# One batch for each group of eight partitions, and rotary tables filled for each tile

## The chip, the cores and the metric

The kernel runs on one core of a Trainium2 chip. The metric is the device time of one execution in microseconds (us); smaller is better. Three timed runs of the kernel before gave 161.45, 161.63 and 161.63 us, median 161.63 us. A difference below about 0.2% can't be told from none here.

The core's engines that matter are VectorE (DVE in the profile), which does all the arithmetic; SyncE (SP), which issues most of the transfers; GpSimd (POOL), which issues three of them; and the 16 DMA engines, which carry every transfer between device memory and the on-chip memory of 128 partitions.

## The reference

The input `x` is float32 of shape (16, 512, 16, 64): batch, position, head, element. Only the first half of each 64-element row is rotated, by a table that depends on the position alone; the second half is passed through.

```python
batch, seq, heads, dim = x.shape            # 16, 512, 16, 64
half_dim = dim // 2                         # 32
x1, x2 = x[..., :half_dim], x[..., half_dim:]
cos = cos[None, :, None, :]                 # (1, 512, 1, 32)
sin = sin[None, :, None, :]
a, b = x1[..., :16], x1[..., 16:]
rotated_first  = a * cos[..., :16] - b * sin[..., :16]
rotated_second = a * sin[..., :16] + b * cos[..., :16]
return np.concatenate([rotated_first, rotated_second, x2], axis=-1)
```

So 33.55 MB are read and 33.55 MB are written, and only the first 16 columns of each table are used.

## The kernel before

**Tiles.** A "run" is K = 16 consecutive positions of one batch: 16 x 16 heads x 64 elements x 4 bytes = 65,536 contiguous bytes. A batch has 32 runs (`PB`). The 512 runs make T = 4 tiles of 128 runs, one run per partition. In the kernel before, run number `128t + p` of the whole input lies in partition `p` of tile `t`, so a tile is one contiguous piece of 8.39 MB: four batches of 32 partitions each. The names `load`, `store` and `rows` move tile `t` (or a range of its 16 positions) to or from slot `t % 3` of `ring`. Three slots hold four tiles: tile 3 goes into slot 0 when tile 0 has been stored.

**Tables.** Position run `r` of a batch needs table run `r` (16 positions x 16 columns, of cos and of sin). GpSimd loads the two tables into every fourth partition of `stage` (lines 63 and 64). `stream_shuffle` (line 73) then spreads them within each group of 32 partitions: partition `32q + j` of `spun` gets table run `8q + (j mod 8)`. Because in this layout every batch occupies 32 partitions in order, partition `p` always needs table run `p mod 32`, whatever the tile. The loop at lines 78 to 80 collects the 32 runs in order in `packed` with four copies, and the loop at lines 82 to 86 writes the table four times (once per group of 32 partitions), with each column pair doubled so that one instruction can multiply 32 columns. This is done once, for all tiles.

**Arithmetic.** `rotate(t, lo, hi)` does positions `lo` to `hi` of a tile with four VectorE instructions: x1 * sin into `b_t` (line 96), x1 * cos in place (line 97), a subtraction (line 98) and an addition (line 101). Half a tile (KC = 8 positions) is one `rotate`; the second half of tile 2 is cut in two at KM = 13.

**Order.** VectorE runs its instructions in program order. SP's queue has, in this order: load 0, load 1, first half of load 2, store 0, second half of load 2, load 3, store 1, store 3. Each waits for what it needs, and holds up those behind it: store 0 for the rotation of tile 0, load 3 for store 0, store 1 for an added dependency on `near`, the first piece of the second half of tile 2. Store 2 goes through GpSimd's queue. All of them are carried by the same 16 DMA engines.

Of the kernel before, what the change touches and what calls it, by code (L numbers as in the profile page):

```python
# [1 line left out]

# [4 lines left out]


@with_exitstack
def kernel(  # L10
    ctx: ExitStack,
    tc: tile.TileContext,
    x: bass.AP,
    cos: bass.AP,
    sin: bass.AP,
    out: bass.AP,
):
    nc = tc.nc
    fp32 = mybir.dt.float32
    P = 128  # L20
    B, S, H, D = x.shape
    Q = D // 4
    HF = D // 2

    K = 16
    T = B * S // (P * K)
    PB = S // K
    REP = P // PB  # L30
    R = H * D
    NS = 3
    KC = K // 2
    KM = 13

    xf = x.rearrange("b s h d -> (b s h d)").rearrange("(t p f) -> t p f", t=T, p=P)
    of = out.rearrange("b s h d -> (b s h d)").rearrange("(t p f) -> t p f", t=T, p=P)
    cosf = cos.rearrange("(p k) j -> p (k j)", k=K)
    sinf = sin.rearrange("(p k) j -> p (k j)", k=K)

    const_pool = ctx.enter_context(tc.tile_pool(name="const", bufs=1))
    b_pool = ctx.enter_context(tc.tile_pool(name="bp", bufs=1, space=bass.MemoryType.PSUM))


    ring = const_pool.tile([P, NS, K, H, D], fp32)
    stage = const_pool.tile([P, 2, K, HF], fp32)
    spun = const_pool.tile([P, 2 * K, Q], fp32)
    packed = const_pool.tile([PB, 2 * K, Q], fp32)
    table = const_pool.tile([P, 2, K, 2, Q], fp32)

    def rows(t, lo, hi):
        return ring[:, t % NS, lo:hi].rearrange("p k h d -> p (k h d)")

    def load(t, lo=0, hi=K):
        return nc.sync.dma_start(out=rows(t, lo, hi), in_=xf[t, :, lo * R : hi * R])

    def store(t, lo=0, hi=K, queue=nc.sync):
        return queue.dma_start(out=of[t, :, lo * R : hi * R], in_=rows(t, lo, hi))  # L58


    nc.vector.memset(stage[:, :, :, 0:Q], 0.0)  # L61
    spread = stage.rearrange("(j b) t k i -> j b t (k i)", b=REP)
    nc.gpsimd.dma_start(out=spread[:, 0, 0], in_=cosf)  # L63
    nc.gpsimd.dma_start(out=spread[:, 0, 1], in_=sinf)  # L64
    load(0)
    load(1)
    load(2, 0, KC)

    PQ = PB // REP
    nc.vector.stream_shuffle(  # L73
        out=spun[:],
        in_=stage.rearrange("p t k j -> p (t k) j")[:, :, 0:Q],
        mask=[j % PQ * REP for j in range(PB)],
    )
    for q in reversed(range(REP)):
        n = PQ * (q + 1)
        nc.vector.tensor_copy(out=packed[0:n], in_=spun[q * PB : q * PB + n])  # L80

    for r in range(REP):
        nc.vector.tensor_copy(  # L83
            out=table[r * PB : (r + 1) * PB].rearrange("p t k c j -> p (t k) c j"),
            in_=packed.unsqueeze(2).to_broadcast((PB, 2 * K, 2, Q)),
        )
    C = table[:, 0].rearrange("p k c j -> p k (c j)")
    Sn = table[:, 1].rearrange("p k c j -> p k (c j)")

    def rotate(t, lo, hi):  # L90
        x1 = ring[:, t % NS, lo:hi, :, 0:HF]
        c = C[:, lo:hi].unsqueeze(2).to_broadcast((P, hi - lo, H, HF))
        s = Sn[:, lo:hi].unsqueeze(2).to_broadcast((P, hi - lo, H, HF))
        b_full = b_pool.tile([P, KC, H, HF], fp32, name="b_t")
        b_t = b_full[:, 0 : hi - lo]
        nc.vector.tensor_mul(out=b_t, in0=x1, in1=s)  # L96
        nc.vector.tensor_mul(out=x1, in0=x1, in1=c)  # L97
        nc.vector.tensor_sub(  # L98
            out=x1[:, :, :, 0:Q], in0=x1[:, :, :, 0:Q], in1=b_t[:, :, :, Q:HF]
        )  # L100
        return nc.vector.tensor_add(  # L101
            out=x1[:, :, :, Q:HF], in0=x1[:, :, :, Q:HF], in1=b_t[:, :, :, 0:Q]
        )

    rotate(0, 0, KC)
    rotate(0, KC, K)
    store(0)
    load(2, KC, K)
    load(3)
    rotate(1, 0, KC)  # L110
    rotate(1, KC, K)
    behind_loads = store(1)
    rotate(2, 0, KC)
    near = rotate(2, KC, KM)
    rotate(2, KM, K)
    store(2, queue=nc.gpsimd)

    tc.add_manual_dep(
        behind_loads.ins,
        near.ins.name,  # L120
        mybir.DependencyInfo(mybir.DependencyClass.Sync, mybir.DependencyReason.DATA),
        reason="the store follows the loads at the DMA engines",
    )
    rotate(3, 0, KC)
    rotate(3, KC, K)
    store(3)


# [1 line left out]
_INS = ['x', 'cos', 'sin']  # L130
_OUTS = [((16, 512, 16, 64), 'float32')]


# [23 lines left out]
```

## Time and profile before

| what | value |
| --- | --- |
| timed runs, median of 3 | 161.63 us |
| the profiled execution, first to last instruction (span) | 159.5 us |
| share of the span in which VectorE is busy | 71% |
| bytes moved, mean rate over the span | 67.24 MB, 422 GB/s |
| VectorE's longest wait for a transfer: for the sin table | 14.4 us |
| VectorE's only wait for a load of `x`: for load 0 | 1.9 us |
| last VectorE instruction (line 101) ends | 131.2 us |
| first rotation starts | 23.0 us |

The page of a profile divides the span by engine and lists groups of instructions, transfers and waits. A "DMA share" is the mean busy share of the 16 DMA engines in a stretch of time; packets are counted where they start, so a short stretch can show more than 1. "To landing" is the time from the issue of a transfer to its completion mark, and holds the time it spent queued behind others. The span is 2.1 us shorter than the timed median; that part lies outside the first and last instruction.

### The profile page before, as it was taken

Reading aid. Unit: us, or ns where it says so; the run is one execution under the profiler, and the core shown is the slowest. Engines: PE = TensorE matmul, PEld = TensorE weight load, DVE = VectorE, ACT = ScalarE, POOL = GpSimd, SP = SyncE. Lnnn points to the kernel's source line nnn. Section 1 sums busy time; section 2 is a strip of 40 time slices with the busy share of each in tenths; the row PEclk is TensorE's granted clock in tenths of the full one; section 3 lists DMA queues with packets and bytes.
Section 4 is the critical chain, followed back from the end, with each engine's and each line's share of the span. In section 5 each row is a group of like instructions: output and inputs, shape, how many; then the busy total and the mean of one; then the engine's idle time right before and its main releaser. Section 6 shows DMA issues by size and latency. Waiting matters only on the chain.

```text
span 159.5 us, 115 instructions
## 1 busy us (share of the span) xinstructions
DVE 112.9 (71%) x47; POOL 1.9 (1%) x7
## 2 busy tenths in 40 slices
DVE  1000959999999999999999999999999990000000
POOL 3000000000000000000000000010000000000000
DMA  7969979899699699699996996996996996998966
GB/s 263 542 263 542 444 345 526 362 427 526 271 493 551 263 526 526 263 395 427 493 526 263 526 526 263 526 526 263 526 526 263 526 510 279 526 427 362 526 263 263
DMA packets 1360, 67.24 MB, mean 422 GB/s; under 512 B 176, under 2 KB 176, under 8 KB 208
## 3 DMA queue, kind: packets, MB, share of 16 engines
q1 hardware_dynamic: 1152, 58.72, 85.7%
q0 software_dynamic: 208, 8.52, 12.4%
HBM read 33.69 MB, written 33.55 MB: 422 GB/s over the span
## 4 chain that ended last, share of the span: by engine, by line
DVE 61%; DMA 14%; issue 5%; DVEq 1%
DVE b_t L96 22%; DVE ring L97 22%; DMA ring<-in_x_dram 14%; DVE ring L101 10%; DVE ring L98 7%; DVEq L152 1%; DVEq L96 0%
## 5 line engine op out<-in xcount | busy, mean ns | idle before, releaser
L96 DVE TENSOR_TENSOR b_t<-ring,table 128x4096 f32<-128x4096 f32 (+2 forms) x9 | 35.6, 3959 | 2.1 <-DMA ring<-in_x_dram 1.9
L97 DVE TENSOR_TENSOR ring<-ring,table 128x4096 f32<-128x4096 f32 (+2 forms) x9 | 35.6, 3950 | 0.3
L98 DVE TENSOR_TENSOR ring<-ring,b_t 128x2048 f32<-128x2048 f32 (+2 forms) x9 | 18.4, 2050 | 0.3
L101 DVE TENSOR_TENSOR ring<-ring,b_t 128x2048 f32<-128x2048 f32 (+2 forms) x9 | 18.4, 2043 | 0.0
L73 DVE LOAD_MASK_SELECT spun<-stage x1 | 0.0, 14 | 14.4 <-DMA stage<-in_sin_dram 14.4
L83 DVE COPY table<-packed 32x1024 f32<-32x1024 f32 x4 | 2.7, 684 | 0.1
L58 POOL DMA_DIRECT2D out_dram<-ring x1 | 0.6, 559 | 101.7 <-DVE ring L101 101.7
L80 DVE COPY packed<-spun 32x512 f32<-32x512 f32 (+3 forms) x4 | 1.7, 416 | 0.1
L61 DVE MEMSET stage<- 128x512 f32 x1 | 0.5, 485 | 0.9 <-PEq L141 0.9
L73 DVE STREAM_SHUFFLE spun<-stage 128x512 f32<-128x512 f32 x1 | 0.7, 722 | 0.0
L63 POOL DMA_DIRECT2D stage<-in_cos_dram x1 | 0.6, 642 | 1.3 <-DVE stage L61 1.3
L64 POOL DMA_DIRECT2D stage<-in_sin_dram x1 | 0.5, 532 | 0.0
L141 POOL MEMSET const-bfloat16-1.0<- 128x1 bf16 x1 | 0.1, 101 | 0.0
L141 POOL MEMSET const-float32-0.0<- 128x1 f32 x1 | 0.1, 98 | 0.2 <-issue 0.2
L141 POOL MEMSET const-float32-1.0<- 128x1 f32 x1 | 0.1, 98 | 0.0
L141 POOL MEMSET const-uint8-127<- 128x1 uint8 x1 | 0.1, 98 | 0.0
## 6 DMA issues: line engine op xcount, KB each, us to landing
ring<-in_x_dram SPq DMA_DIRECT2D x2, 4096.0 KB, 40.7
stage<-in_cos_dram POOLq DMA_DIRECT2D x1, 64.0 KB, 8.9
stage<-in_sin_dram POOLq DMA_DIRECT2D x1, 64.0 KB, 13.3
ring<-in_x_dram SPq DMA_DIRECT2D x3, 28.9
out_dram<-ring SPq DMA_DIRECT2D x3, 27.4
out_dram<-ring POOLq DMA_DIRECT2D x1, 39.5
```

The costliest lines, as they stand in the source:

```text
L58: return queue.dma_start(out=of[t, :, lo * R : hi * R], in_=rows(t, lo, hi))
L61: nc.vector.memset(stage[:, :, :, 0:Q], 0.0)
L63: nc.gpsimd.dma_start(out=spread[:, 0, 0], in_=cosf)
L64: nc.gpsimd.dma_start(out=spread[:, 0, 1], in_=sinf)
L73: nc.vector.stream_shuffle(out=spun[:], in_=stage.rearrange("p t k j -> p (t k) j")[:, :, 0:Q], mask=[j % PQ * REP for j in range(PB)],)
L80: nc.vector.tensor_copy(out=packed[0:n], in_=spun[q * PB : q * PB + n])
L83: nc.vector.tensor_copy(out=table[r * PB : (r + 1) * PB].rearrange("p t k c j -> p (t k) c j"), in_=packed.unsqueeze(2).to_broadcast((PB, ...
L96: nc.vector.tensor_mul(out=b_t, in0=x1, in1=s)
L97: nc.vector.tensor_mul(out=x1, in0=x1, in1=c)
L98: nc.vector.tensor_sub(out=x1[:, :, :, 0:Q], in0=x1[:, :, :, 0:Q], in1=b_t[:, :, :, Q:HF])
L101: return nc.vector.tensor_add(out=x1[:, :, :, Q:HF], in0=x1[:, :, :, Q:HF], in1=b_t[:, :, :, 0:Q])
L152: with _tile.TileContext(nc) as tc:
```

## The change

The distribution of the runs over the partitions changes. Partition `8b + i` of tile `t` now holds run `8t + i` of batch `b`: each tile holds eight runs of all 16 batches, and eight neighbouring partitions belong to one batch. Seen from device memory, a tile is no longer one piece of 8.39 MB but 16 pieces of 524,288 bytes, whose starts lie 2,097,152 bytes apart. The transfer's pattern on the memory side has an outer count of 16 and an inner count of 8, where it had one count of 128.

Tile `t` now needs table runs `8t` to `8t + 7`, repeated in every group of eight partitions. That is what `spun` holds in its partitions `32t` to `32t + 31`. The copies into `packed` are dropped, and `fill(t)` copies the quarter of `spun` that tile `t` needs into all four groups of 32 partitions of a table; two tables take turns. `fill(0)` and `fill(1)` stand ahead of the first rotation, `fill(2)` after store 1, `fill(3)` after store 2. KM goes from 13 to 9, so the instruction that store 1 waits for, `near`, does one position instead of five.

```diff
-    KM = 13
+    KM = 9
 
-    xf = x.rearrange("b s h d -> (b s h d)").rearrange("(t p f) -> t p f", t=T, p=P)
-    of = out.rearrange("b s h d -> (b s h d)").rearrange("(t p f) -> t p f", t=T, p=P)
+    xf = x.rearrange("b (t i k) h d -> t b i (k h d)", t=T, k=K)
+    of = out.rearrange("b (t i k) h d -> t b i (k h d)", t=T, k=K)
...
-    packed = const_pool.tile([PB, 2 * K, Q], fp32)
-    table = const_pool.tile([P, 2, K, 2, Q], fp32)
+    table = const_pool.tile([P, 2, 2, K, 2, Q], fp32)
...
-        return nc.sync.dma_start(out=rows(t, lo, hi), in_=xf[t, :, lo * R : hi * R])
+        return nc.sync.dma_start(out=rows(t, lo, hi), in_=xf[t, :, :, lo * R : hi * R])
...
-        return queue.dma_start(out=of[t, :, lo * R : hi * R], in_=rows(t, lo, hi))
+        return queue.dma_start(out=of[t, :, :, lo * R : hi * R], in_=rows(t, lo, hi))
...
-    for q in reversed(range(REP)):
-        n = PQ * (q + 1)
-        nc.vector.tensor_copy(out=packed[0:n], in_=spun[q * PB : q * PB + n])
-
-    for r in range(REP):
-        nc.vector.tensor_copy(
-            out=table[r * PB : (r + 1) * PB].rearrange("p t k c j -> p (t k) c j"),
-            in_=packed.unsqueeze(2).to_broadcast((PB, 2 * K, 2, Q)),
-        )
-    C = table[:, 0].rearrange("p k c j -> p k (c j)")
-    Sn = table[:, 1].rearrange("p k c j -> p k (c j)")
+    def fill(t):
+        for q in range(REP):
+            nc.vector.tensor_copy(
+                out=table[q * PB : (q + 1) * PB, t % 2].rearrange(
+                    "p t k c j -> p (t k) c j"
+                ),
+                in_=spun[t * PB : (t + 1) * PB]
+                .unsqueeze(2)
+                .to_broadcast((PB, 2 * K, 2, Q)),
+            )
 
     def rotate(t, lo, hi):
         x1 = ring[:, t % NS, lo:hi, :, 0:HF]
+        C = table[:, t % 2, 0].rearrange("p k c j -> p k (c j)")
+        Sn = table[:, t % 2, 1].rearrange("p k c j -> p k (c j)")
...
+    fill(0)
+    fill(1)
     rotate(0, 0, KC)
...
     behind_loads = store(1)
+    fill(2)
     rotate(2, 0, KC)
...
+    fill(3)
     rotate(3, 0, KC)
```

In the program as built, VectorE's eight copies of `fill(2)` and `fill(3)` stand between the rotations of tiles 1 and 2, and all eight stand ahead of `near`. The number and the order of the transfers on SP's and GpSimd's queues are as before.

## The prediction

> **What bounds the kernel now.** I read the page's parts 1 and 3 first: who is busy, and how full the transfer engines are.
>
> ```profile
> span 159.5 us, 115 instructions
> ...
> DVE 112.9 (71%) x47; POOL 1.9 (1%) x7
> ...
> q1 hardware_dynamic: 1152, 58.72, 85.7%
> q0 software_dynamic: 208, 8.52, 12.4%
> ...
> out_dram<-ring SPq DMA_DIRECT2D x3, 27.4
> out_dram<-ring POOLq DMA_DIRECT2D x1, 39.5
> ```
>
> The two queues' packets fill 85.7 + 12.4 = 98.1% of 16 engines' span: 156.5 of 159.5 us. VectorE is busy for 71%. So the DMA engines are the bound, and only 3.0 us of the span (start and end) are not theirs. One tile's transfer (8.39 of the 58.72 MB that took 0.857 x 159.5 = 136.7 us) costs 19.5 us alone. The last row shows what sharing costs: store 2 ran beside store 1 on the same engines and took 39.5 us from issue to landing.
>
> Then the rate by stretches, each with its start and end, busy time of DVE and POOL, the clock, the DMA share and GB/s:
>
> ```profile
> 22.00:51.00 29.00, 27.80 (x9) 0.00 (x0) 1.00 1.00 434
> 51.00:72.00 21.00, 20.86 (x6) 0.00 (x0) 1.00 1.00 424
> ...
> 101.00:132.00 31.00, 29.92 (x11) 0.56 (x1) 1.00 1.02 440
> 132.00:144.00 12.00, 0.00 (x0) 0.00 (x0) 1.00 1.01 437
> ```
>
> Loads alone (first row), store 0 (second) and stores from two queues (the last two) all go at 424 to 440 GB/s with the engines full: some 27 GB/s for each of 16, whatever the direction. Something fixed on each engine's path sets that pace. A faster kernel would need it to rise, or the 3.0 us to shrink.
>
> Last the timeline (start, duration, engine, line), for VectorE's table work and its slack:
>
> ```profile
> 16.56 1.77 DVE L80 COPY packed<-spun 32x512 f32<-32x512 f32 x4
> 18.36 2.78 DVE L83 COPY table<-packed 32x1024 f32<-32x1024 f32 x4
> 22.99 4.43 DVE L96 TENSOR_TENSOR b_t<-ring,table 128x4096 f32<-128x4096 f32 x1 [1.85 <-DMA ring<-in_x_dram]
> ...
> 98.86 32.68 SPq L58 DMA_DIRECT2D out_dram<-ring  x2
> ...
> 104.58 0.56 POOL L58 DMA_DIRECT2D out_dram<-ring  x1 [101.70 <-DVE ring L101]
> ```
>
> VectorE has its table 1.85 us before load 0 is in, and store 1 is issued at 98.86 us, 2 us before the loads ahead of it are done (the second store of that row is store 3, at 131.2 us).
>
> **The change, part by part.**
>
> Tables ahead of the first rotation: four copies into `packed` and four into `table` go (16.56 to 21.14, 4.6 us); eight of the second kind come, at 2.78 / 4 = 0.695 us with its gap, 5.6 us. They end at 22.1 us, still before load 0 (22.9). Cost nothing; cover left 0.8 us. If load 0 came at once, the price would be 1.0 us.
>
> `fill(2)` and `fill(3)`: eight copies more, 5.6 us on VectorE, all ahead of `near`. Against that `near` shrinks from five positions to one. The multiplications take 4.433 us for 4096 elements and 1.767 for 1536, so 1.04 ns an element and 0.17 fixed; 512 elements take 0.70. The additions (2.287 for 2048, 0.953 for 768) give 0.42 for 256. So `near` takes 2 x 0.70 + 2 x 0.42 + gaps, 2.3 us, instead of 98.86 - 90.22 = 8.6. Store 1 would be issued at 98.86 + 5.6 - 6.3 = 98.1 us: not later. The cut of tile 2 costs nothing in sum, with the same instructions and the same elements. Store 3 is issued 5.6 us later, at 136.8; stores 1 and 2 keep the engines full until 144, so that is hidden by about 7 us. Behind it on SP's queue stands only the end. At an unchanged transfer pace VectorE's additions are all covered; with no cover they are 6.6 us, which makes 168.
>
> Issuing: the same five loads and four stores in the same order, with a pattern of two counts. No row shows such an issue. SP's rows are 0.33 to 0.43 us each; I bound the change by -0.1 and +0.4 us apiece and take +0.2. Only load 0's is ahead of everything; later ones lie under transfers under way. POOL's issue (0.56 us) is bounded alike, and lies under store 1.
>
> Transfers: the same bytes in the same packets of 65,536, but each DMA engine gets one outer entry of 16, thus partitions 8b to 8b+7 and one batch. No row shows that assignment's pace. From below: no dearer, 19.5 us a tile. A gain beyond that is excluded by the engines being full at one pace in every stretch, except at the start (load 0 took 22.2 us against 19.5; a gain of 1 us there is the most I allow). From above: if engines meet pairwise on one path to the partitions, each pair shares as stores 1 and 2 shared engines (39.5 us for a tile): twice 19.5 everywhere. Between ends so far apart, the question is whether the 27 GB/s belong to the engine or to the group of partitions it reaches. I take the latter, as a judgement: the pace is the same for reading device memory and for writing it, which puts the limit at the other end of the path or in the engine; it is that of an assignment in which no engine stands in another's way; and no engine has idle time from which a new one could be better.
>
> [...]
>
> **Sum for the likeliest case.** 2 x 156.5 = 313 us if all pairs meet all the time. Less what falls out of step. Engines receive their work within one issue, 0.43 us, against 9.8 us for four packets (half a tile): 4% apart at the start, 6 us saved. And where load 3 and store 2 are under way together (two tiles, 39 us of work, 78 doubled), one engine may read while its partner writes; I take a third of that stretch's 39 us loss as saved, 13 us, between bounds of 0 and 39. So 313 - 6 - 13 = 294 in transfers, 3.0 us start and end, 2.1 us outside the span (161.63 - 159.5): 299 us. Its own range is 255 to 318: above, nothing saved (313 + 5.1); below, pairs that are out of step for four tenths of the work, 156.5 x (0.6 x 2 + 0.4) + 5.1 = 255. VectorE doesn't bind: load 0 lands at about 41 instead of 22.4, and from there VectorE's 113 + 6.6 us of work lie in 300.
>
> **The rivals.**
>
> Pairs fall out of step. One engine of a pair is favoured and gets its first four packets through alone; its partner is then half a tile behind, and they use different partition groups from there on. For it: nothing forces two engines to stay in step. Against it: both have equal work and start within 0.43 us. Price: 9.8 us once, 171 us, when they never meet again; 8 x 9.8 = 78 us, 240, when each of eight tile transfers begins in step. Middle 205. A milder loss elsewhere, as in device memory with its batches 2,097,152 bytes apart, would fall in the same stretch.
>
> The pace is the engine's own. Then partition neighbours don't matter, and what is left is VectorE's covered additions and 0.2 us of issue: 161.8 us, between 160.6 (the start gains 1 us) and 162.5. For it: the equal pace with one queue or two, loads or stores, is what an engine-bound kernel shows as well. Against it: nothing in the profile; it needs the path to any group of partitions to carry two engines' streams, 54 GB/s. From that rate on it decides. That the descriptor side ignores the new pattern and keeps the old assignment has the same price. This is the case on the other side: not slower.
>
> VectorE becomes the bound. Its work begins when load 0 is in (22.9) and ends 108.3 us later now (131.2); with 5.6 more, store 3 is issued at 136.8 and its 19.5 us end at 156.3 at the earliest, under the present 159.5. So only the 168 of lost covers, 2%, counted in the range of the first rival.
>
> **How the numbers follow.** Paired engines 0.70; out of step or a milder loss (163 to 255) 0.20; the engine's own pace 0.10. The predicted time is the first's, 299 us. The range reaches down to 195 and up to 322: that leaves out the last case (0.10), the lower part of the second (0.06) and a little above. A difference under 0.2% can't be told from none: of the last case's 0.10, 0.04 go to faster, 0.03 to within 0.2%, 0.03 to slower. So faster 0.04, same 0.03, slower 0.93.
>
> **What would show it.** Load 0's landing, and with it the first rotation: near 41 us for pairs in step, near 32 for one half late, 23 for no loss. The mean rate over the span: about 226 GB/s (67.24 MB in 297 us) against 422, with the DMA share still near 1, since engines that wait for a path count as busy. VectorE's share near 40%, with long waits for loads. The table copies should be sixteen of 0.68 us, and `near` about 2.3 us long. It is wrong if load 0 lands as before, or if the rate falls in the stores alone, which would put the loss in device memory's writes and not in the partitions.

## The result, and the profile after

The changed kernel takes 289.45 us (median of 6 runs, 285.83 to 295.25) against 161.63. Two of the six runs (290.25 and 295.25) count as slow, over 1.5% above the fastest, so the ratio is taken from the other four (mean 287.8 us): 1.78, 95% interval 1.773 to 1.788. The predicted time was 299 us. The profiled execution took 289.96 us, 288.2 of them in the span.

From the page of the changed kernel, parts 1, 3, 5 and 6 (busy time and share of the span; packets, MB and share of 16 engines; the groups of instructions; microseconds from issue to landing at the end):

```profile
DVE 119.5 (41%) x55; POOL 1.9 (1%) x7
...
DMA packets 1361, 67.25 MB, mean 233 GB/s; under 512 B 176, under 2 KB 176, under 8 KB 208
...
q1 hardware_dynamic: 1152, 58.72, 89.3%
q0 software_dynamic: 208, 8.52, 7.6%
...
L96 DVE TENSOR_TENSOR b_t<-ring,table 128x4096 f32<-128x4096 f32 (+2 forms) x9 | 35.6, 3959 | 84.0 <-DMA ring<-in_x_dram 83.8
...
L79 DVE COPY table<-spun 32x1024 f32<-32x1024 f32 x16 | 11.0, 684 | 0.4
...
out_dram<-ring SPq DMA_DIRECT2D x3, 67.5
```

The same bytes in as many packets (65,536 bytes each, 32,768 for the halves of load 2), and the engines' packets still fill 96.9% of the span (89.3 + 7.6). So the engines hardly rest; each packet takes longer (5.0 to 5.1 us against 2.42 in loads alone). VectorE, whose share fell from 71% to 41%, now waits 83.8 us for loads where it waited 1.9. Its work rose by 6.6 us, as worked out (119.5 against 112.9).

By stretches of the changed kernel (start and end, length, DVE and POOL busy, clock, DMA share, GB/s):

```profile
5.00:100.00 95.00, 47.91 (x25) 0.00 (x0) 1.00 0.99 206
105.00:155.00 50.00, 25.55 (x12) 0.00 (x0) 1.00 1.01 233
160.00:175.00 15.00, 13.89 (x8) 0.14 (x1) 1.00 0.99 210
175.00:207.00 32.00, 0.00 (x0) 0.41 (x1) 1.00 0.97 311
207.00:232.00 25.00, 24.77 (x8) 0.00 (x0) 1.00 1.07 352
235.00:285.00 50.00, 0.00 (x0) 0.00 (x0) 1.00 0.91 201
```

Loads alone (first row) go at 206 GB/s, less than half of 434 before; stores from SP's queue alone (last row) at 201. The second row is store 0 and then the second half of load 2, one behind the other in SP's queue. From 175 us, when store 2 is issued on GpSimd's queue, to 207, when load 3 lands, a load and a store are under way from two queues, at 311. From 207 to 232, when store 2 lands, only stores 1 and 2 are under way, still from two queues, and it is 352. In the trace 216 of the 240 packets of 65,536 bytes that start in the first stretch last 5.0 to 5.1 us, against 2.42 before; of those in the two stretches with two queues, 29 of 152 and 59 of 134 last 2.42 to 2.45 again.

Last the chain of waits of the changed kernel (start, length, what) and the first piece of tile 2 that store 1 waits for:

```profile
0.74 44.36 DMA ring<-in_x_dram
```

```profile
160.50 0.70 DVE L96 TENSOR_TENSOR b_t<-ring,table 128x512 f32<-128x512 f32 x1 [29.68 <-DMA ring<-in_x_dram]
...
162.74 0.59 SPq L57 DMA_DIRECT2D out_dram<-ring  x1
```

Load 0 takes 44.4 us from issue to landing (22.2 before; the prediction had 41), and `near` takes 162.74 - 160.50 = 2.2 us; the 2.3 of the prediction were right, but VectorE had stood still for 29.7 us before it.

### The profile page after: what moved, and what is told of

Its sections match the earlier page's. It is cut to its first block, busy times and chain, and to the rows that moved or that the text cites. A ratio compares the mean times of both kernels' runs of the same rounds, so it can differ in the third digit from the quotient of the medians.

```text
span 288.2 us, 123 instructions
## 1 busy us (share of the span) xinstructions
DVE 119.5 (41%) x55; POOL 1.9 (1%) x7
## 3 DMA queue, kind: packets, MB, share of 16 engines
q1 hardware_dynamic: 1152, 58.72, 89.3%
## 4 chain that ended last, share of the span: by engine, by line
DVE 38%; another core or an unknown queue 26%; DMA 15%; issue 1%; DVEq 1%
DMA ring<-in_x_dram 15%; DVE b_t L96 12%; DVE ring L97 12%; DVE ring L98 6%; DVE ring L101 5%; DVE table L79 2%; DVEq L156 1%; DVEq L96 0%
## 5 line engine op out<-in xcount | busy, mean ns | idle before, releaser
L96 DVE TENSOR_TENSOR b_t<-ring,table 128x4096 f32<-128x4096 f32 (+2 forms) x9 | 35.6, 3959 | 84.0 <-DMA ring<-in_x_dram 83.8
L101 DVE TENSOR_TENSOR ring<-ring,b_t 128x2048 f32<-128x2048 f32 (+2 forms) x9 | 18.4, 2043 | 0.0
L79 DVE COPY table<-spun 32x1024 f32<-32x1024 f32 x16 | 11.0, 684 | 0.4
```

What stands on the lines that cost most here:

```text
L79: nc.vector.tensor_copy(out=table[q * PB : (q + 1) * PB, t % 2].rearrange("p t k c j -> p (t k) c j"), in_=spun[t * PB : (t + 1) * PB] .un ...
L101: return nc.vector.tensor_add(out=x1[:, :, :, Q:HF], in0=x1[:, :, :, Q:HF], in1=b_t[:, :, :, 0:Q])
```

## The experiments

Three theories were kept apart. P: two DMA engines that work on the same group of partitions share one path. M: memory addresses 2 MiB apart, read in step, are slow. D: a memory pattern of two counts is slow as such. Two more came up on the way. N: partitions that aren't an engine's own are slow by themselves. C: enough meetings slow all engines that are under way, also those that meet nobody. The profile doesn't name the engine of a packet, so which engine serves which partitions is inferred from the patterns and the times throughout.

**1. The assignment without the memory gaps.** Kernel before, tile in one piece; only which neighbouring run goes where is changed.

```diff
-    xf = ....rearrange("(t p f) -> t p f", t=T, p=P)
+    xf = ....rearrange("(t i g f) -> t g i f", t=T, i=8, g=16)
```

(`of` alike, and one index more in `load` and `store`.)

> The kernel before with one edit: within a tile, which stays one contiguous piece of 8.39 MB, partition 8g+i holds run 16i+g, so the memory side has counts 16 and 8, each DMA engine gets eight neighbouring partitions, and the 16 engines in step read 16 neighbouring runs, 65,536 bytes apart. The table is that of before, so the rotation multiplies by table rows of other positions. Theory P (pairs of engines meet at one path to a group of partitions): packets of 5.0 us as in the changed kernel, load 0 landing near 45 us, 275 to 300 us in all. Rival M (the loss is in device memory, from pieces 2,097,152 bytes apart): gone, 161 to 163 us. Rival D (a pattern of two counts is slow as such): as P, 275 to 300.

Measured: 289.21 us (288.08 to 289.79), ratio 1.789, interval 1.785 to 1.793. One row of its stretches:

```profile
5.00:100.00 95.00, 46.58 (x23) 0.00 (x0) 1.00 0.99 206
```

206 GB/s again, with no gap in memory. M alone is out. VectorE's table work is here that of before, so the tables are not needed for the loss either.

**2. Gaps in memory without the assignment.**

```diff
-    xf = ....rearrange("(t p f) -> t p f", t=T, p=P)
+    xf = ....rearrange("(g t i f) -> t g i f", t=T, i=4, g=32)
```

> The kernel before with one edit: partition 4g+i of tile t holds run 16g+4t+i, so the memory side has counts 32 and 4, and a tile is 32 pieces of 262,144 bytes whose starts lie 1,048,576 bytes apart. I expect 32 outer entries over 16 engines to give each engine two groups of four partitions, as in the kernel before. The table is that of before, so the rotation multiplies by table rows of other positions. Theory P: no pair meets, 161.3 to 162.5 us, load 0 landing near 22.5 us. Rival M: runs that engines read in step are now 1 MiB apart, well above 161.6, some 200 us or more. Rival D: 275 to 300 us, since this pattern has two counts as well.

Measured: 164.19 us (163.54 to 165.04), ratio 1.015, interval 1.012 to 1.018. Its stretches of loads alone, then of store 0, load 2's second half and load 3:

```profile
5.00:50.00 45.00, 30.52 (x18) 0.00 (x0) 1.00 1.00 425
55.00:100.00 45.00, 44.62 (x16) 0.00 (x0) 1.00 1.03 433
```

Two counts and gaps of 1 MiB, yet 425 to 433 GB/s: D falls. That each engine has two groups of four partitions here and in the kernel before is the author's assumption; what the runs show is the pace, 424 to 434 GB/s in the like stretches of the kernel before. The time lies 1.7 us above the range that P gave. Load 0's wait ended at 24.4 us against 23.0, and the three first issues took 1.95 us against 1.33; what the rest of the 2.6 us is wasn't tried.

**3. The tables alone.** The changed kernel with the layout of before (`xf`, `of` and their indices put back).

> The changed kernel with the two lines of the layout put back to those of before: fill for each tile, two tables, KM = 9, tiles of 128 consecutive runs. The rotation multiplies by table rows of other positions. As predicted, the 6.6 us that VectorE has more are covered: 161.6 us, within 0.3; the first rotation starts at 23 us, store 1 is issued near 98.1 us, store 3 near 136.8 us, and the last transfer still ends near 158.5 us. Rival T (the tables cost what they take): 166 to 168 us.

Measured: 162.58 us (162.48 to 162.64), ratio 1.0061, interval 1.0049 to 1.0074. The additions were not wholly covered: 1.0 us came through. Of its timeline, the row of stores 1 and 3 (start of the first issue, length to the end of the last; experiments 4 and 5 show the same row of theirs):

```profile
98.33 39.08 SPq L57 DMA_DIRECT2D out_dram<-ring  x2
```

Store 1 was issued at 98.3 and store 3 at 137.1 us, as worked out (98.1 and 136.8). The eight late copies lie among the instructions of tiles 1 and 2 here (the first starts at 50.08 us, ahead of tile 1's first rotation, the last at 95.38), not between the two tiles; all are ahead of `near`.

**4. Without the late fills.** Run 3 without `fill(2)` and `fill(3)`.

```diff
-    fill(2)
...
-    fill(3)
```

> The run with the tables alone (layout of before), without fill(2) and fill(3): tiles 2 and 3 multiply by the table rows of tiles 0 and 1. VectorE has 5.6 us less ahead of store 3. If the 1.0 us that the tables cost comes from store 3's late issue (137.4 us, after store 1 had landed at 125.6 and SP's queue had run dry, with first packets of 3.2 to 3.5 us), store 3 is issued near 131.8 and the time is back at 161.6 within 0.3. If it comes from KM = 9 and the earlier issue of store 1, it stays at 162.5 or above.

Measured: 163.01 us (162.37 to 163.40), ratio 1.0081, interval 1.0060 to 1.0102.

```profile
92.44 39.08 SPq L57 DMA_DIRECT2D out_dram<-ring  x2
```

Taking the copies away gave nothing back, for store 1 was then issued 6.4 us earlier than before, at 92.4.

**5. The same with KM = 13.**

```diff
-    KM = 9
+    KM = 13
```

> The tables alone without the late fills (layout of before, fill(0) and fill(1) only; tiles 2 and 3 multiply by the table rows of tiles 0 and 1), and KM back at 13: store 1 issued near 98.9 us instead of 92.4. If the 1.4 us of the run without late fills came from the early issue of store 1, it is 161.6 us within 0.3; if from the eight copies ahead of the first rotation, or from the placement of tables, 162.5 or above.

Measured: 161.56 us (161.38 to 161.75), ratio 1.0005, interval 0.9996 to 1.0014.

```profile
98.86 32.68 SPq L57 DMA_DIRECT2D out_dram<-ring  x2
```

So the eight copies ahead of the first rotation cost nothing, and issuing store 1 at 92.4 instead of 98.9 us costs 1.4 us by itself. In run 3, where store 1 was in time, the 1.0 us must come from the late fills or from the later stores 2 and 3 (store 2 was issued at 110.5 us instead of 104.6). Its trace shows store 1 landed at 125.6 us, nothing left in SP's queue until 137.1, and store 3's first packets at up to 3.50 us instead of 2.42. That this is the cause is argued, not isolated. There are sixteen such packets at 139 us, as many as there are engines, of 3.1 to 3.5 us, some 0.8 us too long each. Run 4 has sixteen of 2.9 to 3.6 us as well, at 97.5 us, where load 3 ends and store 1 follows in a queue that hadn't run dry; run 5 and the kernel before have none at either place. These packets would account for 0.8 us of either loss, but an empty queue doesn't explain both.

**6. Probe of assignment and meetings.** Eight loads, one at a time, ahead of the kernel before; `xr` is the list of 65,536-byte runs, `x32` the same by batches (`nc.sync.` is left out ahead of each `dma_start`).

```python
after_last(dma_start(out=slot, in_=xr[0:128]))
after_last(dma_start(out=slot, in_=xr[0:4].unsqueeze(0).to_broadcast((32, 4, K * R))))
after_last(dma_start(out=slot, in_=xr[0:8].unsqueeze(0).to_broadcast((16, 8, K * R))))
after_last(dma_start(out=slot[0:32], in_=x32[0:8, 0:4]))
after_last(dma_start(out=slot[64:96], in_=x32[0:8, 0:4]))
after_last(dma_start(out=slot[0:36], in_=x32[0:9, 0:4]))
after_last(dma_start(out=slot[0:64], in_=x32[0:8, 0:8]))
after_last(dma_start(out=slot[0:32], in_=x32[0:4, 0:8]))
```

> The kernel before with eight loads into slot 2 ahead of its own, each issued when the one before it has landed; packets of 65,536 bytes throughout, and the output is that of before. Fast means 2.42 us a packet, slow about 5. Step 1, 128 partitions, 128 neighbouring runs: fast, some 21 us (8 packets an engine and 2 us of latency). Step 2, the assignment of before (counts 32 and 4), all groups reading the same four runs. Step 3, the assignment of the change (counts 16 and 8), all engines reading the same eight runs. Theory P (meeting at the partitions): step 2 fast, 21 us; step 3 slow, 42. Rival M (memory addresses): 2 and 3 alike, since in both all engines read the same addresses in step. Step 4, eight engines, partitions 0-31, batches 2 MiB apart: fast, 12 us, by P; slow, 21, by M. Step 5, the same into partitions 64-95: 12 us by P; 21 us if a group of partitions that isn't the engine's own is slow by itself (rival N). Step 6, nine engines, partitions 0-35, where only the first and the ninth meet (0-3 with 32-35): by P seven engines end near 12 us and two near 21; if one meeting slows all that are under way (rival C, which the head-start run suggests), all nine end near 21. Step 7, eight engines, eight partitions each, 0-63: 42 us by P and C. Step 8, four engines, eight partitions each, 0-31, no meeting: 21 us by P and C, 40 by N.

The timeline of SP's queue (start of each issue and its length). Each step is issued when the one before has landed, so the difference of two starts is a step's time:

```profile
0.74 0.39 SPq L84 DMA_DIRECT2D ring<-in_x_dram  x1
23.05 0.67 SPq L86 DMA_DIRECT2D ring<-in_x_dram  x1
45.08 0.58 SPq L91 DMA_DIRECT2D ring<-in_x_dram  x1
88.14 0.80 SPq L95 DMA_DIRECT2D ring<-in_x_dram  x1
100.67 0.70 SPq L96 DMA_DIRECT2D ring<-in_x_dram  x1
113.51 0.81 SPq L97 DMA_DIRECT2D ring<-in_x_dram  x1
136.15 0.63 SPq L98 DMA_DIRECT2D ring<-in_x_dram  x1
179.50 0.65 SPq L99 DMA_DIRECT2D ring<-in_x_dram  x1
202.00 22.35 SPq L55 DMA_DIRECT2D ring<-in_x_dram  x3
```

Step 1 takes 22.3 us, 2.9 more than eight packets of 2.42, where the expectation added 2. In steps 2 and 3 the same few addresses are read over and over; counts of 32 and 4 take 45.08 - 23.05 = 22.0 us, those of the change 43.1. The addresses differ too (four runs read 32 times, eight runs 16 times); experiment 7 has a pair with nothing but the partitions changed. Step 4 (partitions 0 to 31) takes 12.5 and step 5 (the same into 64 to 95) 12.8 us, so N falls; step 8 (22.5, eight packets on each of four engines) agrees. Step 7, which by P has eight engines in four meeting pairs, takes 43.4. In step 6 the completion marks (microseconds after the issue, from the trace) are

```
12.2 12.3 12.4 12.4 12.5 12.6 12.8 | 22.2 22.6
```

nine marks for nine outer entries, taken here as one for each engine: seven early and two late. Step 4, without the ninth, took 12.5 us in all, so the late ones come with the ninth, in partitions 32-35; that they are the ninth itself and the engine in 0-3 is the expectation's assumption, which the marks don't show. The seven others are not slowed (12.2 to 12.8 us).

**7. Partitions against pitch.** Nine groups of three transfers, 16 packets each. `spans(first, step, pitch)` names 16 partitions and 16 runs that are `pitch` runs apart.

```python
behind([go(out=o, in_=i) for o, i in spans(11, 7, 1)])
behind([go(out=o, in_=i) for o, i in spans(0, 8, 1)])
behind([go(out=o, in_=i) for o, i in spans(11, 7, 16)])
behind([go(out=o, in_=i) for o, i in spans(11, 7, 32)])
behind([go(out=o, in_=i) for o, i in spans(0, 8, 32)])
...
```

(The four groups of stores follow in the order of the expectation.)

> The kernel before with nine groups of three transfers ahead of its own; a group is issued when the one before has landed, each transfer is one packet of 65,536 bytes on each of the 16 engines, and the output is that of before. Two choices of partitions: 11, 18, 25, ..., 116 (step 7), where by the groups of partitions that the first probe showed no two engines should meet, and 0, 8, 16, ..., 120 (step 8), where each engine meets another. Memory addresses in step: 65,536 bytes, 1 MiB or 2 MiB apart. Fast means some 10 us from the first issue to the last landing, slow some 17. Loads in the order of their lines: step 7, 64 KiB; step 8, 64 KiB; step 7, 1 MiB; step 7, 2 MiB; step 8, 2 MiB; then stores: step 7, 64 KiB; step 8, 64 KiB; step 7, 2 MiB; step 8, 2 MiB. Theory P alone: step 7 fast and step 8 slow, whatever the addresses. P together with M (16 engines in step 2 MiB apart are slow in memory too, which would explain the head-start run): step 7 at 2 MiB slow as well, some 17 us, and step 8 at 2 MiB no slower than that. M alone fell with the first probe.

Its timeline, read as in the probe before (first issue of each group):

```profile
0.74 1.87 SPq L95 DMA_DIRECT2D ring<-in_x_dram  x3
11.37 1.78 SPq L96 DMA_DIRECT2D ring<-in_x_dram  x3
29.22 1.78 SPq L97 DMA_DIRECT2D ring<-in_x_dram  x3
39.48 1.77 SPq L98 DMA_DIRECT2D ring<-in_x_dram  x3
50.15 1.77 SPq L99 DMA_DIRECT2D ring<-in_x_dram  x3
68.55 2.54 SPq L100 DMA_DIRECT2D out_dram<-ring  x3
77.63 3.83 SPq L101 DMA_DIRECT2D out_dram<-ring  x3
94.69 2.52 SPq L102 DMA_DIRECT2D out_dram<-ring  x3
103.76 3.83 SPq L103 DMA_DIRECT2D out_dram<-ring  x3
```

| group | partitions 11, 18, 25, ... | partitions 0, 8, 16, ... |
| --- | --- | --- |
| loads, 64 KiB apart | 10.6 us | 17.9 us |
| loads, 1 MiB apart | 10.3 us | |
| loads, 2 MiB apart | 10.7 us | 18.4 us |
| stores, 64 KiB apart | 9.1 us | 17.1 us |
| stores, 2 MiB apart | 9.1 us | 17.2 us |

(The last group's end is not marked by an issue; its last completion mark in the trace, at 120.9 us, stands for it.) The two columns of a row have the same addresses and as many packets for each engine. The partitions decide, in both directions; the pitch changes the time by 0.5 us at most. P with M falls. This is the clearest pair of the study.

**8. A head start for twelve engines.** The changed kernel with three loads more at the front. This ran before experiment 6.

```diff
+    for g, lo in ((12, 32), (8, 96), (4, 80)):
+        nc.sync.dma_start(
+            out=ring[lo : lo + 4 * g, 2].rearrange("p k h d -> p (k h d)"),
+            in_=xf[3, 0:g, 0:4],
+        )
```

> The changed kernel with three transfers more, ahead of load 0: pieces of x of 12, 8 and 4 batches, four runs each, into slot 2, where load 2 overwrites them later. On top of the same work, engines 0 to 3 get 12 packets more, 4 to 7 get 8, 8 to 11 get 4, 12 to 15 none (6.3 MB more in all), so that the two engines of each supposed pair start load 0 four packets apart. Theory P: with the pairs out of step, packets of loads 0 to 2 take 2.4 us instead of 5.0, and the first half of load 2 lands near 79 us instead of 105.2, though engines 0 to 3 have moved 32 packets by then instead of 20; load 0 lands near 50 instead of 45. The engines then run dry and fall into step again with store 0, so that the rest stays slow: 255 to 275 us in all. Rivals M and D: packets stay at 5.0 us, the first half of load 2 lands 20 to 60 us later than 105, over 300 us in all.

Measured: 309.7 us (309.17 to 310.34). A miss: the first of the added loads needed 20 to 23 us for four packets on each engine, though by theory P no two engines of this load should meet, and load 2's first half landed at 127.2. But in its stretches:

```profile
5.00:45.00 40.00, 6.21 (x10) 0.00 (x0) 1.00 1.10 213
...
70.00:95.00 25.00, 2.25 (x1) 0.00 (x0) 1.00 0.98 328
```

Between 70 and 95 us loads alone went at 328 GB/s in the changed kernel's own layout, from one queue and in one direction, against 206 without the head start. Pairs out of step would explain it; which engines were out of step the trace doesn't show. Something else had slowed the first added load.

**9. A head start for four engines,** in the layout of run 1.

```diff
+    for m in range(4):
+        nc.sync.dma_start(
+            out=ring[4 + m : 29 + m : 8, 2].rearrange("p k h d -> p (k h d)"),
+            in_=xf[3, 0:4, m],
+        )
```

> The run with neighbouring runs (eight partitions to an engine, memory 64 KiB apart), and ahead of load 0 four transfers of one packet on engines 0 to 3 alone, into partitions 4+m, 12+m, 20+m, 28+m, where no other engine should be working then. So engines 0 to 3 start load 0 four packets later than 4 to 7, and their pairs are out of step; engines 8 to 15 stay in step. The table is that of before, so the rotation multiplies by table rows of other positions. Theory P: load 0's 16 completion marks fall apart into four near 24 us (engines 4 to 7), four near 34 (0 to 3) and eight near 45 (8 to 15); for the first half of load 2 near 53, 63 and 105. The end hangs on engines 8 to 15: 283 to 295 us in all. If being in step doesn't matter, all marks stay near 45 and 105, the first four engines' some 10 to 20 us later.

Measured: 290.95 us (290.66 to 291.25), in the range, but the marks of load 0 were twelve from 46.5 to 47.6 us and four from 61.0 to 61.7. Four late marks fit engines 0 to 3, which had four packets more. Engines 4 to 7, which by P were out of step with their partners, are then among the twelve and were as slow as 8 to 15, in step. Experiment 8 had suggested theory C, and experiment 6 had ruled it out for one pair only; this second miss brought it back for more.

**10. How many meetings.** Six loads, one at a time.

```python
after_last(dma_start(out=slot[32:80], in_=x32[0:12, 0:4]))
after_last(dma_start(out=slot[0:36], in_=x32[0:9, 0:4]))
after_last(dma_start(out=slot[0:40], in_=x32[0:10, 0:4]))
after_last(dma_start(out=slot[0:44], in_=x32[0:11, 0:4]))
after_last(dma_start(out=slot[0:48], in_=x32[0:12, 0:4]))
after_last(dma_start(out=slot[0:64], in_=x32[0:16, 0:4]))
```

> The kernel before with six loads into slot 2 ahead of its own, one at a time, four packets of 65,536 bytes on each engine used, engine e writing four neighbouring partitions; the output is that of before. By the groups found so far: first 12 engines, partitions 32-79, no two meet; then 9 engines, 0-35, one pair meets and 7 engines are alone; 10 engines, 0-39, two pairs and 6 alone; 11 engines, 0-43, three pairs and 5 alone; 12 engines, 0-47, four pairs and 4 alone; 16 engines, 0-63, eight pairs. The head-start runs showed engines slowed that should have been alone while eight others met. Theory P: in every load the engines that are alone end near 12 us, those that meet near 21. Theory C (enough meetings slow all that are under way): from some number of pairs on, the engines that should be alone end near 21 us too, at the latest with four pairs; the first load, without a meeting, ends near 12 us for all.

Its timeline, read as before:

```profile
0.74 0.96 SPq L84 DMA_DIRECT2D ring<-in_x_dram  x1
14.31 0.80 SPq L85 DMA_DIRECT2D ring<-in_x_dram  x1
36.90 0.78 SPq L86 DMA_DIRECT2D ring<-in_x_dram  x1
59.66 0.80 SPq L87 DMA_DIRECT2D ring<-in_x_dram  x1
82.33 0.79 SPq L88 DMA_DIRECT2D ring<-in_x_dram  x1
105.26 0.62 SPq L89 DMA_DIRECT2D ring<-in_x_dram  x1
```

The completion marks after each issue, from the trace:

```
12 engines, no pair      12.6 to 13.6, all twelve
 9 engines, one pair     12.3 to 12.9, seven;  21.7 22.6
10 engines, two pairs    21.2 to 22.7, all ten
11 engines, three pairs  21.4 to 22.7, all eleven
12 engines, four pairs   21.2 to 22.9, all twelve
16 engines, eight pairs  21.4 to 22.7, all sixteen
```

The pairs are counted as the expectation counts them; the marks don't say which engines meet. With nine outer entries two engines are late, with ten all ten, also the six that by that count meet nobody: C holds, from the tenth engine on. The nine engines were in partitions 0-35 both times, so that the number of pairs decides, and not which pair it is, isn't shown. The first load here has the shape and the partitions of the first added one of experiment 8: alone it takes 12.6 to 13.6 us, there it took 20 to 23. There engines 12 to 15, which had no part in it, could begin load 0 beside it. If at least two of them met engines of the added load, C would account for the miss; this was not measured.

**11. Stores on another queue.** `store` in the changed kernel, and as a control in the kernel before.

```diff
-    def store(t, lo=0, hi=K, queue=nc.sync):
+    def store(t, lo=0, hi=K, queue=nc.scalar):
```

> The changed kernel with stores 0, 1 and 3 on ScalarE's transfer queue instead of SP's, so that loads don't wait behind stores in one queue and loads and stores are under way together for longer. Theory P with the step of the prediction that one engine may write partitions while its partner reads them: the mixed stretches run at 300 GB/s or more instead of 220, and the whole takes 240 to 275 us. Rival M, or a limit that doesn't tell the directions apart: 285 to 295 us, as the changed kernel.

Measured: 280.85 us (279.89 to 283.86), ratio to before 1.741, interval 1.733 to 1.748.

```profile
5.00:72.00 67.00, 33.05 (x19) 0.00 (x0) 1.00 0.99 205
72.00:125.00 53.00, 29.95 (x13) 0.00 (x0) 1.00 0.99 292
155.00:200.00 45.00, 3.55 (x2) 0.55 (x1) 1.00 1.01 361
235.00:275.00 40.00, 0.14 (x1) 0.00 (x0) 1.00 0.99 210
```

Where loads and stores were under way together (second and third row) 292 to 361 GB/s passed, and 205 to 210 where there was only one kind. The stretches are as theory P had them; the time lies between the two ranges and in neither, some 7 us below the changed kernel's 287.8, and the last store still ran alone. But the fast stretches differ from the others in a second way: their work comes from two or three queues. The changed kernel's own trace tells the two apart: 352 GB/s from 207 to 232 us, with two stores from two queues and no load. Run 1, with the same assignment, moved 355 in the like stretch (208 to 232 us). So opposite directions aren't needed for the gain; whether they add to it isn't shown.

> The same edit on the kernel before, as a control for the queue alone: engines are full at 27 GB/s each, so 161 to 164 us, no gain.

The control took 166.7 us (165.91 to 167.08), ratio 1.032, interval 1.029 to 1.035: slower, above the range given. So another queue is no gain in itself. But in this layout packets last as long from two queues as from one (in the kernel before all 321 packets of 65,536 bytes that start between 105 and 155 us, 193 of SP's queue and 128 of GpSimd's, last 2.42 to 2.45 us), so the control doesn't tell what a second queue does in the changed layout. Why it lost 5 us wasn't tried.

## Why the prediction was right

**What bounds the kernel.** Right. The DMA engines were full before and after (98.1% and 96.9% of the span), and no edit tried here had a lower median than 161.56 us (experiment 5). The measured loss is in how long a packet takes: 2.42 us before, 5.0 to 5.1 in the changed kernel's loads.

**The pace belongs to the partitions, not to the engine.** The decisive choice, and right, though the prediction made it as a judgement that the profile before couldn't settle: same addresses, other partitions, 10.6 against 17.9 us (experiment 7), and, with addresses that differ as well, 22.0 against 43.1 (6); same partitions, addresses 64 KiB to 2 MiB apart, 10.6, 10.3 and 10.7 us (7). That the engines of the changed layout meet in pairs was the author's judgement, with no row behind it. No run shows which engines meet; what the runs show is the time: 16 partitions that lie eight apart take 1.7 times as long in loads, and 1.9 in stores, as 16 that lie seven apart (7), and loads in the changed layout go at 206 GB/s against 434.

**The sum.** The terms were mis-sized and their errors nearly cancelled; that the sum came within 10 us of 289.45 is partly luck.

- Doubling: predicted 313 us; at the 206 GB/s of loads alone, 67.24 MB take 326, since a packet of these loads takes 2.1 times as long (5.0 to 5.1 us against 2.42) and not 2. That all pairs meet all the time, which the 313 rests on, no run shows; they show those 206 GB/s.
- Out of step: predicted 6 us saved. In loads alone nothing was: of the 240 packets of 65,536 bytes that start between 5 and 100 us none is shorter than 4.8 us. From 105 to 155 us SP's queue moved 11.7 MB, which at 206 would have taken 57 us instead of 50; whether engines out of step saved these 7 us isn't shown.
- Opposite directions: predicted 13 us saved where load 3 and store 2 are under way together, with bounds of 0 and 39. In that stretch, 175 to 207 us, 32 x 311 GB/s are 10.0 MB, which at 206 would have taken 48 us: 16 saved. The size was nearly right, but the reason given, one engine reading while its partner writes, is not what the runs show: the next 25 us, with two stores and no load, were faster still (8.8 MB, 43 us at 206) and saved another 18, which the sum had put at nothing. Both stretches have work from two queues. Why two queues go faster wasn't tried.

So 326 - 7 - 16 - 18 = 285, against 294 predicted; with the 3.0 us of start and end that is 288, and 288.2 were in the span, 1.8 outside it.

**The tables.** Their sizes were right (sixteen copies of 0.684 us, `near` 2.2 us, store 1 and 3 within 0.4 us of the times worked out for the old layout), and in the changed kernel they vanish in VectorE's 83.8 us of waiting. "All covered" was wrong at the old pace: the step that hid store 3's delay behind stores 1 and 2 missed 1.0 us (3). The two stores kept the engines at work until 140 us, past the issue of store 3, as predicted, but store 3 then began with sixteen packets of 3.1 to 3.5 us instead of 2.42; why stays open. The eight copies at the front were covered, as predicted (161.56 against 161.51 us, experiment 5).

**The rivals.** Falling out of step did not happen by itself in loads alone (no packet under 4.8 us). Experiment 10 suggests a reason, which wasn't tried: from ten engines on all were equally slow (21.2 to 22.9 us), so that none got ahead. That engines four packets apart use different groups of partitions no run shows; after such head starts loads went at 328 GB/s in one stretch (8), and there was no gain in the other case (9, 290.95 us against 289.21 in run 1). A loss from addresses 2 MiB apart isn't seen: 10.7 us against 10.6 at 64 KiB (7). That the pace is the engine's own fell with experiments 6 (22.0 against 43.1 us) and 7 (10.6 against 17.9). VectorE never became the bound: it waited 83.8 us for loads.

## What to carry to other kernels

In the probes a load of 9, 10, 11, 12 or 16 outer entries left as many completion marks (experiments 6 and 10), which fits one engine for each entry; which partitions an engine serves the trace doesn't name. Tiles moved as sixteen entries of eight runs took 1.78 times the time, with loads at 206 GB/s; loads and single stores as 32 entries of four, or with a single count of 128, went at 424 to 434 GB/s. When a transfer of 128 partitions runs at half its pace with the DMA share still near 1, as here (206 GB/s at a share of 0.99), look at the length of single packets and at the pattern before suspecting memory: try the same partitions with other addresses, and the same addresses with other partitions.

## What was not expected of the hardware

With nine engines in partitions 0-35 two were late (21.7 and 22.6 us) and the other seven were not (12.3 to 12.9); with a tenth in 36-39 all ten were slow (21.2 to 22.7). From there on it doesn't grow: eleven, twelve and sixteen engines took 21.2 to 22.9 us. What the engines share isn't shown.

In the changed layout work from a second queue went faster: 352 GB/s with two stores from two queues, 292 to 361 with loads and stores from two or three, against 201 to 233 from one queue in the rows shown (328 in one stretch after the head start, experiment 8). Why is open.

Issuing a store 6.4 us too early cost 1.4 us in a kernel bound by its transfers (163.01 against 161.56 us), and stores on a queue of their own cost 5 us (166.7 against 161.6).
